# Gated attention output turned by transposing transfers; merge weights staged two column tiles at a time, the output weight in whole rows

## The chip, the cores and the metric

One core of one Trainium2 chip. The metric is the device time in microseconds (us) of one execution of the whole program. The engines are PE (TensorE), DVE (VectorE), ACT (ScalarE), POOL (GpSimd) and SP, which here only issues transfers. SP and POOL each issue their transfers in order from one queue: what stands behind a transfer that still waits for a semaphore waits too.

## The reference

One layer for 2048 prompt tokens and 8 x 4 sample tokens, 1024 wide, float32. The part around the change:

```python
h = rmsnorm(x, g_pre); proj = h @ w_in          # q k v z_a r glu z_b g_a g_b
o, s_new = gla_chunked(q, k, v, log_a, s0)      # 4 heads, dk 128, dv 256
o = rmsnorm(o, g_gla).reshape(bsz, t_len, 1024) # per head, gain of 256 values
y_a = (o * silu(z_a)) @ w_a_out
...                                             # causal depthwise conv, layernorm
y_b = (cv * silu(z_b)) @ w_b_out
merged = sigmoid(g_a) * y_a + sigmoid(g_b) * y_b
x = x + merged @ w_o
x = x + sigmoid(x @ w_pg) * (p @ w_pe)
```

## The kernel before

Matrix products run in float16 with every operand split in a high and a low half, three products for one (`mm3`, lines 263 to 268: high x high, high x low, low x high). A weight comes from memory as float32 into a staging tile `st`, ACT writes the high half (scaled) and DVE the low half (`load_w`, lines 217 and 218).

The stages, in the order of the source:

- Phase 0: x is normalised and turned by PE into `xT` (lines 366 to 371), and the forget gates are computed and stored to `b_d`.
- Attention: four heads one after the other (`gla_head`), each in nine segments, eight of 256 prompt tokens and one of the 32 sample tokens. A head loads six weight tiles (`wq`, `wk`, four `wvz`). A segment projects q, k, v and z, forms the block scores, and multiplies. The normalised, gated output `zz` (line 1069) has tokens on the partitions. PE turns it into PSUM in four 128 x 128 pieces against the identity matrix (line 1075), ACT and DVE scale it by the gain `gsc` and split it into `at` (lines 1079 and 1080), and two stores on POOL's queue write it to `a_d`, which is laid out channel first.
- Convolution: eight channel tiles (`conv_channels`) begin at set segments (`CPOS`); the taps are a long run of DVE instructions (line 504), of lowest priority.
- Fill: 24 gate projections (`gate_w`, `gate_proj`), 120 blocks of 24 matmuls `fl<-xT,wf`, of a priority below the attention. They go to `zz_d`, `ta_d` and `tb_d` and only have to be there when the merge reads them.
- Merge: ten blocks of 208 tokens. For each of eight column tiles, 24 matmuls with `wA` (w_a_out) on `aT`, 24 with `wB` (w_b_out) on `bT`, then DVE multiplies by the gates and adds into `mT`. `load_a` brings `aT` from `a_d`, eight loads for a block into twelve buffers.
- Output: eight pairs of 128-token tiles are multiplied by w_o, and then by w_pg (`halves`). Both weights are used in seven Strassen-like forms of two groups each (`load_forms`): B11, B21, B22 and the sums T1 to T4. For w_o DVE adds the sums in place (line 259); for w_pg accumulating transfers on POOL's queue add them (line 240). `x_d<-x`, the store of the new x, is on POOL's queue too, and the next x is loaded into one of four buffers `x`, so it waits for the store of the x two pairs back.

The order on each engine is not written by hand. A scheduler places the instructions by priorities (`later`) and by its own expected times, and the order is then fixed; within it each engine runs in order. The staging tiles come from one pool:

```python
wst = ctx.enter_context(tc.tile_pool(name="wst", bufs=4))   # tiles of 128 x 1024 float32
```

Of the kernel before, what the change touches and what calls it, by code (L numbers as in the profile page):

```python
# [89 lines left out]
def hybrid_step(ctx: ExitStack, tc, A, O):  # L90
# [2 lines left out]

    cpool = ctx.enter_context(tc.tile_pool(name="const", bufs=1))
    stat = ctx.enter_context(tc.tile_pool(name="stat", bufs=2))
    wst = ctx.enter_context(tc.tile_pool(name="wst", bufs=4))
    wpool = ctx.enter_context(tc.tile_pool(name="wpool", bufs=8))
    slab_ctx = ExitStack()
    slab = slab_ctx.enter_context(tc.tile_pool(name="slab", bufs=8, reuse_waits="tile"))
# [4 lines left out]
    def sb_pool(name, bufs):  # L104
        return tc.tile_pool(name=name, bufs=bufs, reuse_waits="tile")

    def dma(out, in_):
        return nc.sync.dma_start(out=out, in_=in_)
# [37 lines left out]
    def small_vectors(pool):  # L146
        rows = pool.tile([38, P], F32, name="rows", bufs=1)
        dma(rows, A["rows"])
        pt = sm_tile()
        PE.transpose(pt[:, 0:38], rows, ident[0:38, 0:38])  # L150
        V.tensor_copy(vec, pt[:, 0:38])
        V.tensor_scalar(out=g_pre, in0=vec[:, 0:8], scalar1=SX * RSF, scalar2=None, op0=MULT)
        with later(2000):
            V.tensor_scalar(out=gln, in0=vec[:, 16:24], scalar1=RSF, scalar2=None, op0=MULT)
            V.tensor_scalar(out=lnh[:, 0], in0=gln, scalar1=0.5, scalar2=None, op0=MULT)
            V.tensor_scalar(out=lnh[:, 1], in0=b_ln, scalar1=0.5, scalar2=None, op0=MULT)
            V.tensor_scalar(out=gsc, in0=vec[:, 36:38], scalar1=SA * 0.5 * IS * RSF * DK ** -0.5, scalar2=None, op0=MULT)
            V.tensor_tensor(out=sel, in0=ident[:, 0:TD], in1=ident[:, TD:2 * TD], op=ADD)
            for g in range(2, 4):
                V.tensor_tensor(out=sel, in0=sel, in1=ident[:, g * TD:(g + 1) * TD], op=ADD)  # L160
            nc.gpsimd.memset(onesd, 1.0 / D)
# [41 lines left out]
    def wdma(out, in_):  # L203
# [3 lines left out]
        with tc.issue_after(xdma[0].ins):  # L207
            return dma(out, in_)

    def load_w(src, c0, width=P, k0=0, nk=KC, pool=None):  # L210

        c0 = [c0] if isinstance(c0, int) else c0
        w = (pool or wpool).tile([P, 2, nk, len(c0) * width], F16, tag="w", name="w")
        st = wst.tile([P, nk, len(c0) * width], F32, tag="st", name="st")
        for i, c in enumerate(c0):
            wdma(st[:, :, i * width:(i + 1) * width], src[k0 * P:(k0 + nk) * P, c:c + width].rearrange("(k p) c -> p k c", p=P))
        S.activation(w[:, 0], st, AF.Copy, scale=SW)
        V.scalar_tensor_tensor(out=w[:, 1], in0=st, scalar=SW, in1=w[:, 0], op0=MULT, op1=SUB)  # L218
        return w

    def load_forms(src, tiles, accum):


        forms = [[None, None] for _ in range(7)]

        def split(f, g, st):
            w = next(tiles)
            S.activation(w[:, 0], st, AF.Copy, scale=SW)
            V.scalar_tensor_tensor(out=w[:, 1], in0=st, scalar=SW, in1=w[:, 0], op0=MULT, op1=SUB)
            forms[f][g] = w  # L230
        yield forms

        def load(g, r, c, st=None):
            r0 = r * 512 + g * 256
            q = src[r0:r0 + 256, c * 512:(c + 1) * 512].rearrange("(k p) c -> p k c", p=P)
            if st is None:
                st = wst.tile([P, 2, 512], F32, tag="st", name="st")
                dma(st, q)
            else:
                nc.gpsimd.dma_start(out=st, in_=q, accum_op=ADD)  # L240
            return st
        for g in range(2):
            if accum:
                for f, r, c in ((B11, 0, 0), (B21, 1, 0), (B22, 1, 1)):
                    split(f, g, load(g, r, c))
                    yield
                st = load(g, 0, 1)
                for f, r, c in ((T3, 1, 1), (T2, 0, 0), (T4, 1, 0)):
                    split(f, g, load(g, r, c, st))
                    yield  # L250
                split(T1, g, load(g, 0, 0, load(g, 0, 1)))
                yield
                continue
            b11, b21, b22, b12 = (load(g, r, c) for r, c in ((0, 0), (1, 0), (1, 1), (0, 1)))
            for f, st in ((B11, b11), (B21, b21), (B22, b22)):
                split(f, g, st)
                yield
            for f, to, frm in ((T3, b22, b12), (T1, b12, b11), (T2, b11, b22), (T4, b21, b11)):
                V.tensor_tensor(out=to, in0=to, in1=frm, op=ADD)
                split(f, g, to)  # L260
                yield

# [32 lines left out]
    ta_d = dram.tile([P, KC, TT], F32, name="ta_d")  # L295
    tb_d = dram.tile([P, KC, TT], F32, name="tb_d")
    b_d = dram.tile([P, NH, TT], F32, name="b_d")
    a_d = dram.tile([P, KC, 2, TT], F16, name="a_d")

    def gate_w(c, which, other=False, early_w=False):  # L300
        base = (C_ZB, C_GA, C_GB)[which]
# [285 lines left out]


    mpool = ctx.enter_context(sb_pool("mpool", T // (2 * P)))
    wpool2 = ctx.enter_context(sb_pool("wpool2", 9))  # L590
    wA = [load_w(A["w_a_out"][0], c * P) for c in range(KC)]
    w_o = []
    mT = []
    p3_ctx = ExitStack()
    p3 = p3_ctx.enter_context(sb_pool("p3", 2))

    def load_a(a, n, aT, _, __):
        for k in range(KC):
            t = p3.tile([P, 2, DB], F16, tag="aT", name="aT", bufs=12)
            dma(t[:, :, 0:n], a_d[:, k, :, a:a + n])  # L600
            aT.append(t)

    load_a(*ops[0])
    wB = [load_w(A["w_b_out"][0], c * P, pool=wpool2) for c in range(KC)]
    for blk, (a, n, aT, bT, _) in enumerate(ops):
        ahead = iter(())
        if blk + 1 < len(ops):
# [44 lines left out]
    with sb_pool("p4", 2) as p4:  # L652
# [8 lines left out]
        def split_forms(t, sc):  # L661

            a11, a12, a21, a22 = (t[:, 4 * k:4 * k + 4, i * P:(i + 1) * P] for i in range(2) for k in range(2))
            sums = [p4.tile([P, 4, P], F32, tag="sum", name="sum", bufs=3) for i in range(3)]
            F = {f: p4.tile([P, 2, 4, P], F16, tag="f", name="f", bufs=10) for f in (A11, A12, S2, S1, S3, A22, S4)}
            hl(F[A11], a11, sc)
            hl(F[A12], a12, sc)
            V.tensor_tensor(out=sums[0], in0=a21, in1=a22, op=SUB)
# [110 lines left out]
        class Gate:  # L779
# [4 lines left out]
                self.n = [0, 0]  # L784

            def keep(self, X, n):
                r = wst.tile([P, 512], F32, tag="st", name="r")
                S.copy(r, X)
                return r

# [77 lines left out]
def gla_head(tc, nc, A, O, h, L):  # L868
# [13 lines left out]
    for a, n in GSEGS:  # L882
# [184 lines left out]
        rs = rsqrt(ms, nck, ck, 1.0 / DV)  # L1067
        for c in range(nck):
            V.scalar_tensor_tensor(out=zz[:, c], in0=po[0:ck, c], scalar=rs[:, c:c + 1], in1=zz[:, c], op0=MULT, op1=MULT)
        at = p2.tile([P, 2, 2, 256], F16, tag="at", name="at")  # L1070
        pt = sm_tile()
        for j in range(2):
            pj = pt[:, j * 256:j * 256 + n]
            for c in range(nck):
                PE.transpose(pj[:, c * ck:(c + 1) * ck], zz[:, c, j * P:(j + 1) * P], ident[0:ck, 0:ck])
        for j in range(2):
            pj = pt[:, j * 256:j * 256 + n]
            g = L["gsc"][:, j:j + 1]
            S.activation(at[:, j, 0, 0:n], pj, AF.Copy, scale=g)
            V.scalar_tensor_tensor(out=at[:, j, 1, 0:n], in0=pj, scalar=g, in1=at[:, j, 0, 0:n], op0=MULT, op1=SUB)  # L1080
            store(L["a_d"][:, 2 * h + j, :, a:a + n], at[:, j, :, 0:n])
        yield


# [41 lines left out]
```

## Time and profile before

| | |
|---|---|
| median of 3 runs (us) | 2454.31 (2452.01 to 2458.31) |
| the profiled execution's own time (us) | 2464.93 |
| its span in the profile (us) | 2463.2 |
| mean granted TensorE clock | 0.983 |
| PE busy, share of the span | 95% |
| DVE / ACT / POOL busy | 68% / 35% / 18% |

The profiled execution lasted 0.43% longer than the median. Busy time of PE counts matmuls whose ends overlap only once, and a row's mean time of one matmul is longer than the distance to the next.

### The profile page before, as it was taken

The page shows a single profiled execution, that of the slowest core. Times are in us where ns is not written, and L with a number is a line of the kernel's source. Part 1 is how long each engine was busy: PE and PEld are TensorE (multiplying, and loading weights), DVE is VectorE, ACT ScalarE, POOL GpSimd, SP SyncE. Part 2 cuts the span into 40 slices and gives each one's busy share as a digit, 9 for nine tenths or more (in the row PEclk, how much of TensorE's full clock was granted, in tenths as well). Part 3 has the DMA queues.
Part 4 walks back from the last instruction along what each step waited for, and adds up shares of the span by engine and source line. Part 5 has one row for each costly group of instructions (what it writes and reads, how often), then busy time and mean ns, then how long its engine had stood idle before and what let it go on. Part 6 is the DMA issues. An engine that isn't in the chain of part 4 may idle for free.

```text
span 2463.2 us, 43458 instructions
## 1 busy us (share of the span) xinstructions
PE 2336.9 (95%) x16909; PEld 1467.2 (60%) x16909; DVE 1676.1 (68%) x3779; ACT 859.7 (35%) x2043; POOL 451.7 (18%) x1023
## 2 busy tenths in 40 slices
PE   5589999998899999999999989999999998999997
PEld 3245565654456655556655556655999997444544
DVE  6476897496594695594775784654577878865666
ACT  6462123323123324123224223443234334423454
POOL 2011203211112122222122222121000000111333
PEclk9799999999999999999999999999999999999999
DMA  5441201104112113211113130245355445742322
GB/s 182 108 145 32 66 27 61 43 10 125 45 48 63 35 33 111 62 36 51 34 51 94 63 81 29 58 123 166 96 128 130 114 111 181 188 142 89 101 80 73
DMA packets 195942, 210.04 MB, mean 85 GB/s; under 512 B 39323, under 2 KB 167641, under 8 KB 194200
## 3 DMA queue, kind: packets, MB, share of 16 engines
q1 hardware_dynamic: 172104, 133.85, 20.9%
q0 software_dynamic: 23632, 73.42, 8.4%
q8 instruction: 132, 2.16, 0.4%
q14 instruction: 74, 0.61, 0.1%
HBM read 138.33 MB, written 69.72 MB: 84 GB/s over the span
## 4 chain that ended last, share of the span: by engine, by line
PE 74%; DVE 8%; DMA 7%; issue 4%; POOL 4%; ACT 2%; SPq 1%; DVEq 0%; POOLq 0%; ACTq 0%
PE mm L266 13%; PE mm L267 13%; PE mm L268 13%; PE fl L266 6%; PE fl L267 6%; PE fl L268 6%; PE mm L685 4%; PE fl L685 3%; POOL ms L198 1%; DVE acc L504 1%; DMA st<-in_w_in 1%; PE sm L1028 1%; PE sm L1030 1%; PE sm L1029 1%; DMA st<-in_w_pg 1%
## 5 line engine op out<-in xcount | busy, mean ns | idle before, releaser
L266 PE MATMUL mm<-xT,w 128*128 128x416 f16 (+2 forms) x1216 | 362.5, 303 | 4.1 <-DVE zz L932 4.1
L268 PE MATMUL mm<-xT,w 128*128 128x416 f16 (+2 forms) x1216 | 362.4, 303 | 1.0 <-DVE w L218 1.0
L267 PE MATMUL mm<-xT,w 128*128 128x416 f16 (+2 forms) x1216 | 362.3, 303 | 0.0
L266 PE MATMUL fl<-xT,wf 128*128 128x416 f16 x960 | 329.9, 344 | 13.2 <-DVE ob L320 11.7
L267 PE MATMUL fl<-xT,wf 128*128 128x416 f16 x960 | 329.8, 344 | 0.0
L268 PE MATMUL fl<-xT,wf 128*128 128x416 f16 x960 | 329.6, 343 | 0.0
L504 DVE SCALAR_TENSOR_TENSOR acc<-ue,kvec,acc 128x1025 f32<-128x1025 f32 (+1 forms) x232 | 293.9, 1294 | 0.0
L267 PEld LDWEIGHTS <-w 128*128 128x128 f16 x2496 | 243.3, 98 | 69.6 <-issue 11.0
L266 PEld LDWEIGHTS <-w 128*128 128x128 f16 x2496 | 243.4, 98 | 63.2 <-issue 5.5
L268 PEld LDWEIGHTS <-w 128*128 128x128 f16 x2496 | 243.3, 98 | 59.5 <-issue 2.5
L685 PEld LDWEIGHTS <-f 128*128 128x128 f16 x1356 | 132.4, 98 | 160.6 <-issue 6.7
L266 PE MATMUL mm<-w,xT 128*128 128x512 f16 x512 | 195.3, 382 | 0.0
L267 PE MATMUL mm<-w,xT 128*128 128x512 f16 x512 | 195.1, 381 | 0.0
L268 PE MATMUL mm<-w,xT 128*128 128x512 f16 x512 | 195.1, 381 | 0.0
L685 PE MATMUL mm<-wf,f 128*128 128x512 f16 (+1 forms) x780 | 180.2, 379 | 7.3 <-ACT f L658 4.3
L266 PE MATMUL fl<-bT,w 128*128 128x208 f16 x640 | 162.5, 254 | 2.0 <-ACT ob L318 2.0
L266 PE MATMUL mm<-aT,w 128*128 128x208 f16 x640 | 161.5, 253 | 2.4 <-DMA aT<-a_d 2.4
L267 PE MATMUL fl<-bT,w 128*128 128x208 f16 x640 | 162.6, 254 | 0.0
L268 PE MATMUL fl<-bT,w 128*128 128x208 f16 x640 | 162.5, 254 | 0.0
L268 PE MATMUL mm<-aT,w 128*128 128x208 f16 x640 | 161.5, 253 | 0.0
L267 PE MATMUL mm<-aT,w 128*128 128x208 f16 x640 | 161.5, 253 | 0.0
L504 DVE SCALAR_TENSOR_TENSOR acc<-acc,ksum 128x1024 f32<-128x1024 f32 x120 | 155.0, 1292 | 0.0
(277 smaller groups left out, 4061.6 us busy)
## 6 DMA issues: line engine op xcount, KB each, us to landing
x<-in_x_prompt SPq DMA_DIRECT2D x32, 512.0 KB, 6.0
stf<-in_w_in SPq DMA_DIRECT2D x48, 256.0 KB, 6.5
st<-in_w_in SPq DMA_DIRECT2D x24, 512.0 KB, 10.4
zz_d<-ob POOLq DMA_DIRECT2D x40, 208.0 KB, 2.8
ta_d<-ob POOLq DMA_DIRECT2D x40, 208.0 KB, 2.3
tb_d<-ob POOLq DMA_DIRECT2D x40, 208.0 KB, 2.6
cv<-cv_d SPq DMA_DIRECT2D x80, 104.0 KB, 2.1
zz<-zz_d SPq DMA_DIRECT2D x80, 104.0 KB, 2.2
```

The lines of the kernel that those rows point to most:

```text
L198: E.tensor_scalar(out=x, in0=x, scalar1=scale, scalar2=EPS, op0=MULT, op1=ADD)
L266: PE.matmul(out, lhsT=lh, rhs=rh, start=(k == 0), stop=False)
L267: PE.matmul(out, lhsT=lh, rhs=rl, start=False, stop=False)
L268: PE.matmul(out, lhsT=ll, rhs=rh, start=False, stop=(k == nk - 1))
L504: V.scalar_tensor_tensor(out=out[:, 0:n], in0=src[:, j:j + n], scalar=w1[:, j:j + 1], in1=out[:, 0:n], op0=MULT, op1=ADD)
L685: PE.matmul(ps[:, c0:c0 + w], lhsT=F[fa][:, p == 2, k], rhs=W[fb][k // 2][:, p == 1, k % 2, c0:c0 + w], start=start and k + p == 0, stop=k ...
L1028: PE.matmul(po[:, c], lhsT=qe[:, cc], rhs=st_prev, start=True, stop=False)
L1029: PE.matmul(po[:, c], lhsT=att[:, c], rhs=v[:, c], start=first, stop=True)
L1030: PE.matmul(pu[:, c * DV:(c + 1) * DV], lhsT=kdT[:, cc], rhs=v[:, c], start=True, stop=True)
```

## The change

1. The gain of the head norm (`gsc`) moves from `at` into w_a_out: `load_pair` scales w_a_out by `SW * g_gla`.
2. `gla_head` no longer turns `zz` on PE. ACT and DVE split it where it is, tokens on partitions, and two stores write it to `a_d`, now laid out token first.
3. `load_a` reads `a_d` with two transposing transfers of 208 x 1024 float16 for a block, on SP's queue, into one tile of two buffers.
4. `load_pair` stages w_a_out and w_b_out 256 columns at a time (1 MB, runs of 1 KB) in four loads each instead of eight.
5. `load_forms` loads 256 whole rows (1 MB) at a time, two for a group. For w_pg the sums that DVE would add in place are built by seven accumulating transfers for a group, where there were four.
6. The staging pool is two tiles of 128 x 2048 instead of four of 128 x 1024; all other loads (`load_w`) use half of such a tile. A buffer pool of its own holds `r` (`Gate.keep`), `f` has nine buffers instead of ten, `wpool2` eight instead of nine.

```diff
-    wst = ctx.enter_context(tc.tile_pool(name="wst", bufs=4))
+    wst = ctx.enter_context(tc.tile_pool(name="wst", bufs=2))
-            V.tensor_scalar(out=gsc, in0=vec[:, 36:38], scalar1=SA * 0.5 * IS * RSF * DK ** -0.5, scalar2=None, op0=MULT)
+            V.tensor_scalar(out=gsc, in0=vec[:, 36:38], scalar1=SW, scalar2=None, op0=MULT)
+    def st_tile():
+        return wst.tile([P, 2 * D], F32, tag="st", name="st")
+
+    def load_pair(src, c0, pool, gains=None):
+        st = st_tile().rearrange("p (k c) -> p k c", k=KC)
+        dma(st, src[:, c0:c0 + 2 * P].rearrange("(k p) c -> p k c", p=P))
+        for i in range(2):
+            w = pool.tile([P, 2, KC, P], F16, tag="w", name="w")
+            si = st[:, :, i * P:(i + 1) * P]
+            for sl, g in [(slice(0, KC), SW)] if gains is None else [(slice(j, KC, 2), gains[:, j:j + 1]) for j in range(2)]:
+                S.activation(w[:, 0, sl], si[:, sl], AF.Copy, scale=g)
+                V.scalar_tensor_tensor(out=w[:, 1, sl], in0=si[:, sl], scalar=g, in1=w[:, 0, sl], op0=MULT, op1=SUB)
+            yield w
...
-        st = wst.tile([P, nk, len(c0) * width], F32, tag="st", name="st")
+        st = st_tile()[:, 0:nk * len(c0) * width].rearrange("p (k c) -> p k c", k=nk)
...
         for g in range(2):
-            if accum:
-                for f, r, c in ((B11, 0, 0), (B21, 1, 0), (B22, 1, 1)):
-                    split(f, g, load(g, r, c))
-                    yield
-                st = load(g, 0, 1)
-                for f, r, c in ((T3, 1, 1), (T2, 0, 0), (T4, 1, 0)):
-                    split(f, g, load(g, r, c, st))
-                    yield
-                split(T1, g, load(g, 0, 0, load(g, 0, 1)))
...
+            b = []
+            for r in range(2):
+                st = st_tile().rearrange("p (k i c) -> p k i c", k=2, i=2)
+                r0 = r * 512 + g * 256
+                dma(st, src[r0:r0 + 256].rearrange("(k p) (i c) -> p k i c", p=P, i=2))
+                b.append([st[:, :, i] for i in range(2)])
+            for f, r, c in ((B11, 0, 0), (B21, 1, 0), (B22, 1, 1)):
+                split(f, g, b[r][c])
+                yield
+            for f, (r, c), more, done in ((T3, (1, 1), ((0, 1),), (0, 1)), (T1, (0, 1), ((0, 0),), (0, 0)),
+                                          (T2, (0, 0), ((0, 1), (1, 1)), (1, 1)), (T4, (1, 0), ((0, 0), (0, 1), (1, 1)), (0, 0))):
+                to = b[r][c]
+                if accum:
+                    for r1, c1 in more:
+                        r0 = r1 * 512 + g * 256
+                        nc.gpsimd.dma_start(out=to, in_=src[r0:r0 + 256, c1 * 512:(c1 + 1) * 512].rearrange("(k p) c -> p k c", p=P), accum_op=ADD)
+                else:
+                    V.tensor_tensor(out=to, in0=to, in1=b[done[0]][done[1]], op=ADD)
+                split(f, g, to)
+                yield
...
-    a_d = dram.tile([P, KC, 2, TT], F16, name="a_d")
+    a_d = dram.tile([TT, 2, D], F16, name="a_d")
...
-        for k in range(KC):
-            t = p3.tile([P, 2, DB], F16, tag="aT", name="aT", bufs=12)
-            dma(t[:, :, 0:n], a_d[:, k, :, a:a + n])
-            aT.append(t)
+        t = p3.tile([P, 2, KC, DB], F16, tag="aT", name="aT", bufs=2)
+        for i in range(2):
+            nc.sync.dma_start_transpose(out=t[:, i], in_=a_d[a:a + n, i])
+        aT.extend(t[:, :, k] for k in range(KC))
...
-        at = p2.tile([P, 2, 2, 256], F16, tag="at", name="at")
-        pt = sm_tile()
-        for j in range(2):
-            pj = pt[:, j * 256:j * 256 + n]
-            for c in range(nck):
-                PE.transpose(pj[:, c * ck:(c + 1) * ck], zz[:, c, j * P:(j + 1) * P], ident[0:ck, 0:ck])
-        for j in range(2):
-            pj = pt[:, j * 256:j * 256 + n]
-            g = L["gsc"][:, j:j + 1]
-            S.activation(at[:, j, 0, 0:n], pj, AF.Copy, scale=g)
-            V.scalar_tensor_tensor(out=at[:, j, 1, 0:n], in0=pj, scalar=g, in1=at[:, j, 0, 0:n], op0=MULT, op1=SUB)
-            store(L["a_d"][:, 2 * h + j, :, a:a + n], at[:, j, :, 0:n])
+        at = p2.tile([P, 2, 2, DV], F16, tag="at", name="at")[0:ck, :, 0:nck]
+        sc = SA * 0.5 * IS * RSF * DK ** -0.5
+        S.activation(at[:, 0], zz, AF.Copy, scale=sc)
+        V.scalar_tensor_tensor(out=at[:, 1], in0=zz, scalar=sc, in1=at[:, 0], op0=MULT, op1=SUB)
+        for i in range(2):
+            store(L["a_d"][a:a + n, i, h * DV:(h + 1) * DV].rearrange("(c p) v -> p c v", c=nck), at[:, i])
```

The scheduler makes a new order of it. Three places follow. First PE, in the last head, where the eighth segment's decayed keys `kd` are turned (`sm` is PSUM); lines 944 and 966 of before are 953 and 975 of the change. Before:

```order
L266 LDWEIGHTS wf
L266 MATMUL fl<-xT_106,wf 128x416
L1075 MATMUL sm<-ident,zz 128x128
L944 MATMUL sm<-ident,kd 128x128
L1075 MATMUL sm<-ident,zz 128x128 x3
L944 MATMUL sm<-ident,kd 128x128
L966 MATMUL sm<-qk 32x48 x8
L966 MATMUL sm<-eq,kf 32x48 x8
```

The same place after the change:

```order
L277 LDWEIGHTS xT_110
L277 MATMUL mm<-w,xT_110 128x512
L953 MATMUL sm<-ident,kd 128x128 x2
L975 MATMUL sm<-qk 32x48 x8
L975 MATMUL sm<-eq,kf 32x48 x16
```

The four matmuls on `zz` are gone, and no other one stands in their place; ahead of the keys now stands a projection of the attention itself (`mm`) and no fill (`fl`). Through the whole program the fill moves back: before, 2675 of the 2880 fill matmuls stand ahead of the last head's final matmul (L1061); after, 2110 do, and 537 of the others stand in one run between the first 96 `aT` matmuls and the first `bT` matmul.

Second SP's queue at the end of the attention, from the last load of a sample state (`s`) on. Before:

```order
L108 DMA s_16902<-in_state_gla 128x4x256
L108 DMA aT<-a_d 128x2x208 x8
L108 DMA st<-in_w_b_out 128x8x128 x3
L108 DMA aT<-a_d 128x2x208 x2
L108 DMA st<-in_w_b_out 128x8x128
L108 DMA aT<-a_d 128x2x208 x2
```

After:

```order
L108 DMA s_16663<-in_state_gla 128x4x256
L609 DMA_TRANSPOSE aT<-a_d 128x8x208 x3
L108 DMA st<-in_w_b_out 128x8x256
L609 DMA_TRANSPOSE aT<-a_d 128x8x208
L108 DMA st<-in_w_b_out 128x8x256
```

Two whole blocks are brought by four transfers where one block and a half were brought by twelve.

Third POOL's queue in the output stage, with the accumulating transfers of w_pg and the stores of x. Before:

```order
L240 DMA st<-in_w_pg 128x2x512 x2
L111 DMA x_d<-x 128x1024
L240 DMA st<-in_w_pg 128x2x512
L111 DMA x_d<-x 128x1024
L240 DMA st<-in_w_pg 128x2x512
L111 DMA x_d<-x 128x1024 x2
L240 DMA st<-in_w_pg 128x2x512 x2
L111 DMA x_d<-x 128x1024 x4
```

After:

```order
L266 DMA st<-in_w_pg 128x2x512 x2
L111 DMA x_d<-x 128x1024
L266 DMA st<-in_w_pg 128x2x512 x5
L111 DMA x_d<-x 128x1024 x3
L266 DMA st<-in_w_pg 128x2x512
L111 DMA x_d<-x 128x1024
L266 DMA st<-in_w_pg 128x2x512 x2
L111 DMA x_d<-x 128x1024 x2
L266 DMA st<-in_w_pg 128x2x512 x4
L111 DMA x_d<-x 128x1024 x3
```

Runs of five and of four accumulating transfers now stand ahead of stores of x; before, no more than two did.

More of the change, by code (lines that the diff above doesn't have):

```diff
@@ L231, in load_forms @@
         yield forms
[L233 to L241, printed above, removed]
-        for g in range(2):
-            if accum:
-                for f, r, c in ((B11, 0, 0), (B21, 1, 0), (B22, 1, 1)):
-                    split(f, g, load(g, r, c))
-                    yield
-                st = load(g, 0, 1)
-                for f, r, c in ((T3, 1, 1), (T2, 0, 0), (T4, 1, 0)):
-                    split(f, g, load(g, r, c, st))
-                    yield
-                split(T1, g, load(g, 0, 0, load(g, 0, 1)))
-                yield
[L253 to L259, printed above, removed]
@@ L589, in hybrid_step @@
     mpool = ctx.enter_context(sb_pool("mpool", T // (2 * P)))
-    wpool2 = ctx.enter_context(sb_pool("wpool2", 9))
-    wA = [load_w(A["w_a_out"][0], c * P) for c in range(KC)]
+    wpool2 = ctx.enter_context(sb_pool("wpool2", 8))
+    wA = [w for c in range(0, KC, 2) for w in load_pair(A["w_a_out"][0], c * P, wpool, gsc)]
     w_o = []
@@ L597, in load_a @@
     def load_a(a, n, aT, _, __):
-        for k in range(KC):
-            t = p3.tile([P, 2, DB], F16, tag="aT", name="aT", bufs=12)
-            dma(t[:, :, 0:n], a_d[:, k, :, a:a + n])
-            aT.append(t)
+        t = p3.tile([P, 2, KC, DB], F16, tag="aT", name="aT", bufs=2)
+        for i in range(2):
+            nc.sync.dma_start_transpose(out=t[:, i], in_=a_d[a:a + n, i])
+        aT.extend(t[:, :, k] for k in range(KC))
     load_a(*ops[0])
-    wB = [load_w(A["w_b_out"][0], c * P, pool=wpool2) for c in range(KC)]
+    wB = [w for c in range(0, KC, 2) for w in load_pair(A["w_b_out"][0], c * P, wpool2)]
     for blk, (a, n, aT, bT, _) in enumerate(ops):
@@ L664, in split_forms @@
             sums = [p4.tile([P, 4, P], F32, tag="sum", name="sum", bufs=3) for i in range(3)]
-            F = {f: p4.tile([P, 2, 4, P], F16, tag="f", name="f", bufs=10) for f in (A11, A12, S2, S1, S3, A22, S4)}
+            F = {f: p4.tile([P, 2, 4, P], F16, tag="f", name="f", bufs=9) for f in (A11, A12, S2, S1, S3, A22, S4)}
             hl(F[A11], a11, sc)
@@ L786, in keep @@
             def keep(self, X, n):
-                r = wst.tile([P, 512], F32, tag="st", name="r")
+                r = p4.tile([P, 512], F32, tag="r", name="r", bufs=3)
                 S.copy(r, X)
```

## The prediction

> **What bounds the kernel now.** I read the page's head first, then the stages, then what PE waits for.
>
> ```profile
> span 2463.2 us, 43458 instructions
> PE 2336.9 (95%) x16909; PEld 1467.2 (60%) x16909; DVE 1676.1 (68%) x3779; ACT 859.7 (35%) x2043; POOL 451.7 (18%) x1023
> ...
> PE 74%; DVE 8%; DMA 7%; issue 4%; POOL 4%; ACT 2%; SPq 1%; DVEq 0%; POOLq 0%; ACTq 0%
> ```
>
> The stages, as stretches of time (busy us of PE, PEld, DVE, ACT, POOL, then clock and DMA): start, attention, its end, merge, output by w_o, output by w_pg.
>
> ```profile
> 0.00:215.00 215.00, 157.23 (x897) 86.62 (x898) 115.82 (x205) 109.77 (x183) 31.73 (x95) 0.91 0.42 128
> 215.00:1580.00 1365.00, 1324.90 (x9371) 780.83 (x9369) 954.15 (x2080) 398.27 (x1102) 294.78 (x686) 0.99 0.19 54
> 1580.00:1720.00 140.00, 135.42 (x940) 78.37 (x939) 76.59 (x217) 63.23 (x149) 29.99 (x70) 0.99 0.46 136
> 1720.00:2060.00 340.00, 336.09 (x3676) 330.89 (x3674) 255.01 (x834) 122.67 (x286) 1.62 (x3) 0.99 0.46 119
> 2060.00:2180.00 120.00, 113.37 (x652) 57.61 (x651) 98.61 (x153) 47.17 (x69) 13.94 (x16) 0.97 0.69 196
> ```
>
> PE is the bound: 97% busy in the attention, 99% in the merge, and three quarters of the chain. So PE work taken away is worth its time; work taken from ACT, DVE or POOL only what PE waited for it. PE is idle 126 us in all, 58 of them in the first 215 us. What it waited for outside the start and near the change:
>
> ```profile
> PE sm L1075 <- DVE zz L1069: 14.6, 8, 2.9
> PE fl L266 <- DVE ob L320: 11.7, 8, 4.0
> PE sm L1052 <- DMA s<-in_state_gla: 9.7, 1, 9.7
> ...
> PE mm L266 <- DMA aT<-a_d: 2.4, 3, 1.4
> ```
>
> **The transposes on PE go.** The group of full segments, and instructions of PE in order of time, two of the fill (`fl`) ahead of four transposes (start us, us):
>
> ```profile
> L1075 PE MATMUL sm<-ident,zz 128*128 128x128 f32 x128 | 25.5, 287 | 14.6 <-DVE zz L1069 14.6
> ...
> 905.80 0.34 PE L267 MATMUL fl<-xT,wf 128*128 128x416 f16 x1
> 905.98 0.34 PE L268 MATMUL fl<-xT,wf 128*128 128x416 f16 x1
> 907.57 0.33 PE L1075 MATMUL sm<-ident,zz 128*128 128x128 f32 x1 [1.25 <-DVE zz L1069]
> 907.73 0.27 PE L944 MATMUL sm<-ident,kd 128*128 128x128 f32 x1
> 907.96 0.55 PE L1075 MATMUL sm<-ident,zz 128*128 128x128 f32 x3
> ```
>
> 128 instructions keep PE busy 25.5 us. Started back to back they cost less: three span 0.55 us and one lasts about 0.27, so the distance is (0.55 - 0.27) / 2 = 0.14 us, and 128 of them 18 us. I take 24, ends 18 and 25.5; the eight small ones of the sample segments are within that.
>
> In front of them PE waited 14.6 us for `zz`, which hangs on POOL's slow reciprocal root. After the change nothing on PE reads `zz`, so the wait itself is gone. Late next are the keys, scores and state matmuls. They ran here behind the transposes, with runs of 20 to 60 fill matmuls as cover; the new order has 565 fewer fill matmuls inside the attention. I take 9 of the 14.6, ends 0 and 14.6.
>
> **ACT and DVE in the attention.** Per full segment two 480 ns splits out of PSUM become one of 512 columns:
>
> ```profile
> L1079 ACT ACTIVATE at<-sm,gsc 128x256 f16<-128x256 f32 x64 | 30.4, 475 | 55.1 <-PE sm L1075 46.2 <-DVE at L1080 8.4
> L1080 DVE SCALAR_TENSOR_TENSOR at<-sm,gsc,at 128x256 f16<-128x256 f32 x64 | 30.7, 480 | 11.9 <-ACT at L1079 11.7 <-ACT zz L931 0.2
> ...
> DVE zz L1069 <- POOL rsq_y L190: 112.2, 31, 6.4
> ...
> L659 DVE SCALAR_TENSOR_TENSOR f<-sum,f 128x512 f16<-128x512 f32 x64 | 42.8, 686 | 0.0
> ```
>
> By the last row (a split of 512 columns elsewhere) DVE goes from 30.7 to 32 x 0.69 = 22 us, ACT alike; both lie beside PE: nothing. POOL still issues two stores of 128 KB a segment. Yet DVE is 954 / 1365 = 70% busy in the attention, and if the same work runs in some 120 us less (565 fill matmuls at the 0.18 us between the two rows above, 100 us, and the transposes), it is near 76%. That is the cover that could fail (second rival).
>
> **The transposing transfers.** No row shows one. The nearest:
>
> ```profile
> aT<-a_d SPq DMA_DIRECT2D x80, 104.0 KB, 2.4
> x<-x_d SPq DMA_DIRECT2D x16, 512.0 KB, 4.2
> st<-in_w_in SPq DMA_DIRECT2D x24, 512.0 KB, 10.4
> ...
> 1697.59 3.99 SPq L108 DMA_DIRECT2D aT<-a_d  x8
> 1694.61 0.71 POOL L111 DMA_DIRECT2D a_d<-at  x1
> ...
> L266 PE MATMUL mm<-aT,w x640: 249/253/253, 1701.8 to 2072.7; 128*128 128x208 f16 x160
> L1061 PE MATMUL sm<-oq,sel x8: 379/391/403, 674.0 to 1681.2; 128*32 128x256 f32 x8
> ```
>
> A transfer now has 416 KB. Bounds: 2.4 us, as the small plain ones, to 10.4 us, as 512 KB in short runs; I take 5, nearest to the 512 KB row with long runs. In the merge a block of PE work lasts about 340 / 10 = 34 us and the next block's two transfers are issued ahead of it, so they hide, and SP's eight issues (3.99 us) fall to two. The 2.4 us that PE waited for the later half of `aT` go.
>
> Exposed is the first block. The first load follows the last store of the attention by 3.0 us and PE starts on `aT` 20.6 us after L1061 (1681.2 to 1701.8). In the new order 74 fill matmuls at 0.18 us, 13 us, lie between the two. The path without the PE transposes is about 4 us shorter than the 16.4 us to the issue, so 12, plus two transfers in turn, 10: 22 us against 13. The fill run may be stretched by some 3 us of evictions; I take +6, ends 0 and +20 (10.4 us each). With the 2.4: +3.6.
>
> The Trainium skill, page "VectorE: DVE Perf Modes", section "The three transpose paths", speaks against the change: 1309 ns for a 128 x 128 block by the DMA crossbar, 390 ns by TensorE. Our row has 287 ns for the PE's. At that price a transfer of 13 such blocks would be an estimated 17 us, and the first block's term some +30 instead of +6. The page "DMA: Bandwidth & Descriptors", section "Latency and other measured facts", gives 261 GB/s for such transfers, an estimated 1.6 us. No run so far shows which holds.
>
> **The staging.** w_a_out and w_b_out come in eight loads of 1 MB instead of sixteen of 512 KB, and are split in as many bytes; w_a_out takes 16 splits of half the width instead of eight, eight more instructions on ACT and on DVE, beside fill: nothing. In phase 0 ACT's queue has the weight splits between those of `xT`, and the third and fourth loads now wait until a staging tile is free:
>
> ```profile
> 78.22 1.06 ACT L217 ACTIVATE w<-st 128x1024 f16<-128x1024 f32 x1 [3.77 <-DMA st<-in_w_in]
> 87.72 1.06 ACT L217 ACTIVATE w<-st 128x1024 f16<-128x1024 f32 x1 [5.87 <-DMA st<-in_w_in]
> 97.88 1.06 ACT L217 ACTIVATE w<-st 128x1024 f16<-128x1024 f32 x1 [6.80 <-DMA st<-in_w_in]
> ```
>
> These waits hold `xT` and PE. Two tiles make the loads later, but the new order puts three splits ahead of the next `xT` instead of four. Taken at 0, ends -5 and +10.
>
> **The output stage.** For w_pg POOL issues 14 accumulating transfers of 512 KB instead of 8; those on one tile follow each other, and the stores of x stand behind them.
>
> ```profile
> 2110.08 1.19 POOL L240 DMA_DIRECT2D st<-in_w_pg  x1 [2.26 <-DVE wf L229]
> 2117.90 0.59 POOL L111 DMA_DIRECT2D x_d<-x  x1 [6.64 <-DMA st<-in_w_pg]
> 2132.16 0.56 POOL L111 DMA_DIRECT2D x_d<-x  x1 [8.06 <-DVE x L765]
> ...
> x_d<-x POOLq DMA_DIRECT2D x16, 512.0 KB, 4.5
> ...
> DVE gfin L655 <- DMA gfin<-in_g_final: 2.9, 1, 2.9
> ```
>
> One that is waited for holds the queue some 8 us (1.19 + 6.64). The run of five has three such waits within its two tiles, about 21 us, so the next store of x comes some 20 us later than here. The load two pairs on needs it; store and load land in 4.5 + 4.2 us, so that x is there 29 us later than it was stored before, and a pair lasts 14 us (2117.90 to 2132.16), two 28: a hole of 0 to 8 us, and a smaller one at the run of four. w_pg itself is due only when the w_o pairs end, 100 us on. Against it the load of `gfin`, for which DVE waits 2.9 us (in a stage where DVE is 98.61 / 120 busy), is issued earlier. I take +3, ends -3 and +20. That two 1 MB tiles of w_o must be free before the second group loads is inside these ends.
>
> **The sum.** -24 - 9 + 3.6 + 0 + 3 = -26.4 us. Against the profiled execution, 2464.93, that is 2438.5; it stands 10.6 us above the median of the three runs (2454.31), so against the median 2428.
>
> **Rivals.**
> - The cover holds better: all 14.6 us go and the first block costs nothing. 18 to 25.5 and 14.6 and 2.4 give 2412 to 2419; with the better ends of phase 0 and output, 2404.
> - The waits come back in the attention: PE, with fewer fill matmuls, waits for DVE and ACT. For it speaks DVE at 76% and the 112.2 us that it waits for POOL's root; against it that PE waits only some 40 us in the attention now. If it loses 12 us, 2440.
> - Staging and POOL take it all: phase 0 at +10, output at +20. 2454.3 - 33 + 3.6 + 30 = 2455: no change. For it: ACT's waits for staged weights above, and the order of POOL; against it: w_pg is due late, and the order of ACT is no worse.
> - Slower: the transfers starve the merge. With T for one transfer, the first block costs 12 + 2T - 13 us and each of nine later blocks 2T - 34 where that is above 0. At T = 17 us the first block takes the whole gain of 33 us and the time is 2454; from there it is slower, at T = 20 us 2454.3 - 33 + 39 + 9 x 6 = 2514. For it: nothing here shows a transposing transfer. Against: 512 KB landed in 4.2 to 10.4 us. The 1309 ns of the Trainium skill's page on VectorE lies just on this edge.
>
> **How the numbers follow.** Runs of this kernel differ by 0.3%, 7 us, about what can be told from no change: faster is below 2447, slower above 2462. The sum 0.56 (2418 to 2438); better 0.08; waits back 0.14, of it 0.12 faster; all taken 0.12, of it 0.09 the same; starved 0.10, of it 0.08 slower. Faster 0.56 + 0.08 + 0.12 = 0.76, same 0.02 + 0.09 + 0.02 = 0.13, slower 0.03 + 0.08 = 0.11. The range 2404 to 2458 leaves out the starved merge and parts of the ends.
>
> **What would show it.** L1075 gone and PE's busy time near 2312 us; PE's wait for `zz` gone and no new one of its size in the attention; DMA_TRANSPOSE landing in about 5 us; a wait of PE for `aT` once, under 10 us; stores of x behind the accumulations by some 20 us. The prediction is wrong if a transfer takes over 15 us, or if PE's idle time grows by more than 15 us.

## The result, and the profile after

The changed kernel takes 2436.78 us (median of six runs, 2430.26 to 2442.99) against 2455.39 us for the kernel before beside it: a ratio of 0.9924, 95% interval 0.9900 to 0.9948, so 19 us less (13 to 25). The prediction was 2428 us in a range of 2404 to 2458. Sign and size came out; the experiments below show that they did so in good part for other reasons than the working gave.

The head of the changed kernel's page (its profiled execution took 2438.05 us, 1.3 above the median):

```profile
span 2436.3 us, 42955 instructions
...
PE 2326.4 (95%) x16773; PEld 1452.8 (60%) x16773; DVE 1670.9 (69%) x3751; ACT 854.3 (35%) x2015; POOL 470.1 (19%) x1029
```

PE's busy time fell by 10.5 us, to 2326.4 and not to the 2312 that the prediction named as its sign, and its idle time by 16.4 (from 126.3 to 109.9). The stages of the changed kernel, busy us of PE, PEld, DVE, ACT, POOL, then clock and DMA; they end earlier than before, and the third now holds the first block of the merge:

```profile
0.00:215.00 215.00, 167.26 (x970) 92.41 (x971) 123.61 (x218) 110.78 (x187) 36.24 (x105) 0.94 0.41 127
215.00:1450.00 1235.00, 1211.18 (x8580) 708.34 (x8578) 925.86 (x1986) 372.27 (x1019) 286.62 (x647) 0.99 0.20 56
1450.00:1600.00 150.00, 137.54 (x1023) 82.15 (x1022) 95.91 (x292) 76.76 (x194) 34.84 (x78) 0.98 0.48 134
1600.00:2040.00 440.00, 439.15 (x4341) 393.54 (x4338) 256.90 (x828) 130.50 (x294) 13.50 (x25) 1.00 0.42 104
2040.00:2160.00 120.00, 107.43 (x504) 45.76 (x505) 96.87 (x143) 45.95 (x68) 22.91 (x25) 0.91 0.78 207
```

In the start PE works 10 us more than before in the same 215 us. Between 1450 and 1600 us it idles 12.5 us, where the kernel before idles 8.0. In the 120 us from the end of the merge on PE is busy for 107 us at a clock of 0.91 (before, from 2075 us on, 113 at 0.97). What PE waited for, all of its larger waits but those of the start:

```profile
PE fl L275 <- DVE ob L329: 10.7, 7, 2.7
...
PE mm L694 <- ACT f L667: 7.7, 1, 7.7
PE fl L275 <- ACT ob L327: 6.9, 1, 6.9
...
PE sm L1052 <- ACT att L1010: 4.7, 2, 4.1
PE mm L694 <- DVE x L774: 4.1, 1, 4.1
...
PE sm L1061 <- DMA s<-in_state_gla: 2.2, 1, 2.2
```

The 14.6 us for `zz` are gone. Longer than before are the waits for one eviction of the fill by ACT (`ob`: 6.9 us, before 2.0) and two in the output stage (for `f` 7.7 us, before 4.3; for `x` 4.1 us at one time, before 1.7 at three). The tile `aT`, its first and last matmul and its transfers (ns, minimum, median and maximum that one held SP's queue), and who waited for them:

```profile
L275 PE MATMUL mm<-aT,w x640: 249/253/253, 1559.1 to 2036.9; 128*128 128x208 f16 x160
...
L609 SPq DMA_TRANSPOSE aT<-a_d x20: 1444/2048/5817, 1553.7 to 1970.7; - x20
...
  PE mm L275: 1.1, 1
...
DMA to landing us min/median/max: 4.1/5.3/9.8
```

They land in 5.3 us in the median, and PE waited 1.1 us for them in all. The merge begins 143 us earlier than before (1559.1 against 1701.8) and in the midst of the fill: 143 us ahead of the fill's end, where it was 30. SP's and ACT's queues there:

```profile
1553.67 6.50 SPq L609 DMA_TRANSPOSE aT<-a_d  x3
1560.28 0.53 SPq L108 DMA_DIRECT2D st<-in_w_b_out  x1
1560.87 5.82 SPq L609 DMA_TRANSPOSE aT<-a_d  x1
```

```profile
1567.73 2.00 ACT L221 ACTIVATE w<-st 128x1024 f16<-128x1024 f32 x2 [9.11 <-DMA st<-in_w_b_out]
...
1588.60 0.38 ACT L574 ACTIVATE bT<-th 128x208 f16<-128x208 f32 x1 [9.27 <-DVE th L571]
...
1591.40 0.49 ACT L327 ACTIVATE ob<-fl 128x416 f32<-128x416 f32 x1
```

ACT stands 9.1 us for a staged weight and 9.3 us for `th`, with the evictions of the fill behind both; the one at 1591.40 is what PE waits 6.9 us for. `th` itself stood on DVE behind a sum that waited for a load of `cv`, the convolution's output for a later block of the merge:

```profile
1587.75 0.38 DVE L538 TENSOR_TENSOR s<-s,cv 128x208 f32<-128x208 f32 x1 [8.02 <-DMA cv<-cv_d]
1588.19 0.38 DVE L571 TENSOR_TENSOR th<-th,zz 128x208 f32<-128x208 f32 x1
```

A load of `cv` lands in 2.1 us in the median; of those issued between 1560 and 1600 us one took 10.7 us, and the two loads of w_o beside them (1 MB each) 15.7 us in the median. The second place is POOL's queue in the output stage:

```profile
2078.48 1.18 POOL L266 DMA_DIRECT2D st<-in_w_pg  x1 [0.33 <-DVE wf L244]
2086.53 1.18 POOL L266 DMA_DIRECT2D st<-in_w_pg  x1 [6.87 <-DMA st<-in_w_pg]
2093.32 1.20 POOL L266 DMA_DIRECT2D st<-in_w_pg  x1 [5.61 <-DMA st<-in_w_pg]
2094.04 1.09 POOL L111 DMA_DIRECT2D x_d<-x  x1
```

The run of accumulations holds the store of x until 2094.04. Counted from the end of the merge that is 12 us later than before (2117.90 us, less the 35.8 us by which the merge ended earlier, is 2082).

### The profile page after: what moved, and what is told of

It reads as the page before. It is cut to its first block, busy times and chain, and to the rows that moved or that the text cites. A ratio compares the mean times of both kernels' runs of the same rounds, so it can differ in the third digit from the quotient of the medians.

```text
span 2436.3 us, 42955 instructions
## 1 busy us (share of the span) xinstructions
PE 2326.4 (95%) x16773; PEld 1452.8 (60%) x16773; DVE 1670.9 (69%) x3751; ACT 854.3 (35%) x2015; POOL 470.1 (19%) x1029
## 4 chain that ended last, share of the span: by engine, by line
PE 76%; DVE 8%; DMA 5%; POOL 5%; issue 3%; ACT 2%; SPq 1%; DVEq 0%; POOLq 0%; ACTq 0%
PE mm L275 13%; PE mm L277 13%; PE mm L276 13%; PE fl L275 6%; PE fl L276 6%; PE fl L277 6%; PE mm L694 6%; PE fl L694 4%; DVE acc L513 2%; DMA st<-in_w_in 2%; DMA stf<-in_w_in 1%; POOL rsq_t L187 1%; PE sm L1038 1%; PE sm L1037 1%; POOL rsq_t L188 1%
## 5 line engine op out<-in xcount | busy, mean ns | idle before, releaser
L275 PE MATMUL fl<-xT,wf 128*128 128x416 f16 x960 | 329.7, 343 | 20.2 <-DVE ob L329 10.7
L513 DVE SCALAR_TENSOR_TENSOR acc<-ue,kvec,acc 128x1024 f32<-128x1024 f32 (+1 forms) x232 | 293.1, 1283 | 0.0
```

The costliest lines, as they stand in the source:

```text
L275: PE.matmul(out, lhsT=lh, rhs=rh, start=(k == 0), stop=False)
L513: V.scalar_tensor_tensor(out=out[:, 0:n], in0=src[:, j:j + n], scalar=w1[:, j:j + 1], in1=out[:, 0:n], op0=MULT, op1=ADD)
```

## Experiments

The differences below are between ratios to the kernel before, times 2455 us; the bounds of a difference of two ratios are put together from their intervals.

**The two halves apart.** The turn alone: parts 1 to 3 of the change, with `load_w` scaling w_a_out and the staging as before. The staging alone: the changed kernel with the turn undone.

```diff
 # turn only, on the kernel before
-    def load_w(src, c0, width=P, k0=0, nk=KC, pool=None):
+    def load_w(src, c0, width=P, k0=0, nk=KC, pool=None, gains=None):
-    wA = [load_w(A["w_a_out"][0], c * P) for c in range(KC)]
+    wA = [load_w(A["w_a_out"][0], c * P, gains=gsc) for c in range(KC)]
 # and gla_head, load_a, a_d, gsc as in the change
```

Expected of the turn alone:

> The kernel before with the turn alone: the gated output is split in its own orientation, stored as rows and turned by the transposing transfers, with the gain in w_a_out; staging stays in four tiles of 4 KB a partition, with the old order of loads and eight accumulations for w_pg. Theory (the turn is the gain, the staging costs about as much in the output stage as it brings in phase 0): the start as before (first matmul on xT near 115 us, not 103), the output stage as before (388 us, not 397), the attention shorter by 18 to 25 us of transposes and some of the 14.6 us of wait: 2425 to 2435 against 2455 for the kernel before, so level with the changed kernel or up to 10 us below. Rival A (a good part of the changed kernel's gain is the earlier start): 2440 to 2448, above the changed kernel. Rival B (staging only costs, nothing in phase 0 is kept): 2415 to 2425.

Expected of the staging alone:

> The changed kernel with the turn put back on PE: transposes, splits out of PSUM, the turned a_d and its plain loads as in the kernel before; the staging stays new (two tiles of 8 KB, column tiles in pairs, whole rows, fourteen accumulations). Theory: first matmul on xT near 103 us instead of 115, output stage near 397 us instead of 388, the two cancel: 2450 to 2460, no change that can be told from the kernel before. Rival A: the earlier start is kept to the end and the output stage costs less than it seems: 2440 to 2448. Rival B: staging only costs: 2460 to 2470.

The turn alone: 2431.34 us, ratio 0.9899 (0.9880 to 0.9917), -25 us. That is in the theory's band, but the start is not as before: the first matmul `mm<-xT,w` comes at 106.7 us, where 115 was expected. The staging alone: 2442.17 us, 0.9945 (0.9929 to 0.9961), -14 us, in the band of its rival A. Both together -19. On the new staging the turn is worth 5 us (±7), which cannot be told from nothing, on the old one 25 (±5). Either half makes a new order (by the traces the staging alone moves over 800 of PE's 16909 matmuls), and in the order of the staging alone PE, which still turns `zz`, waits for it much less:

```profile
PE sm L1084 <- DVE zz L1078: 4.4, 5, 1.5
```

**What a transpose on PE costs.** The turn put back on PE in vain, beside the transfers; and, on the kernel before, each transpose issued three times.

```diff
 # turn twice, on the changed kernel
+        pt = sm_tile()
+        for j in range(2):
+            pj = pt[:, j * 256:j * 256 + n]
+            for c in range(nck):
+                PE.transpose(pj[:, c * ck:(c + 1) * ck], zz[:, c, j * P:(j + 1) * P], ident[0:ck, 0:ck])
 # three times, on the kernel before
+                for _ in range(3):
                     PE.transpose(pj[:, c * ck:(c + 1) * ck], zz[:, c, j * P:(j + 1) * P], ident[0:ck, 0:ck])
```

> The changed kernel with the old transposes of the gated output put back on PE into a PSUM tile that nobody reads: the transfers turn the output, as in the changed kernel, and PE does so too in vain. Theory (what the change saves is PE's work on the transposes, 18 to 25 us, and PE's wait for the gated output in front of them, up to 14.6 us): 20 to 35 us slower than the changed kernel, 2457 to 2472, with the wait of PE for zz back at 10 to 15 us. Rival (the matmuls behind had to wait for other things anyway, so that the transposes were free): under 12 us slower.

> The kernel before with each of the 136 transposes of the gated output issued three times into the same place: 272 more on PE, no new wait. It prices a transpose on PE. By the spacing of 0.14 us between transposes issued back to back: +37 us (2493). By the mean duration of one, 0.2 us: +53 us. Rival (most of them stand in time in which PE waits anyhow, as putting them back in vain cost 5 us in place of 18): +10 to +20 us.

In vain: 2441.66 us, 0.9943 (0.9928 to 0.9959), 5 us (±7) above the changed kernel; the rival held. Three times: 2488.47 us, 1.0139 (1.0119 to 1.0159), +34 us (±5). The page's line of PE there:

```profile
PE 2363.5 (95%) x17181; PEld 1495.8 (60%) x17181; DVE 1676.3 (67%) x3779; ACT 859.4 (35%) x2043; POOL 435.9 (18%) x1023
```

272 more transposes are 34 us of time, 0.125 us each, and 26.6 to 29.4 us of PE's busy time (against the two profiles of the kernel before), 0.10 to 0.11 us each. So by this run the 136 of the kernel before cost 13 to 17 us (up to 20 with the interval), and the 37 us that the spacing of 0.14 us gave lie within the interval. The run in vain shows a third of it: 5 us (±7) of time, and PE's busy time only 0.9 us above the changed kernel's. But it is not the changed kernel with more work. By the traces over 2000 of PE's matmuls stand elsewhere in it than in the changed kernel, and its merge begins at 1666.8 us, not at 1559.1. So it does not price the transposes; the three-fold run has a new order too (some 750 matmuls moved), so its price is the better one and still not a clean one.

**The kernel before once more, and two tiles.** To see whether the waits of the first profile were chance; and the kernel before with two staging tiles for the column tiles and nothing else.

```diff
 # two tiles, on the kernel before
-    wst = ctx.enter_context(tc.tile_pool(name="wst", bufs=4))
+    wst = ctx.enter_context(tc.tile_pool(name="wst", bufs=2))
+    wsf = ctx.enter_context(sb_pool("wsf", 2))        # opened at the merge
-                st = wst.tile([P, 2, 512], F32, tag="st", name="st")
+                st = (wsf if c else wst).tile([P, 2, 512], F32, tag="st", name="st")
-                r = wst.tile([P, 512], F32, tag="st", name="r")
+                r = wsf.tile([P, 512], F32, tag="st", name="r")
```

> The kernel before, unchanged, for a second profile of it and for what two timings of one program can differ by. So far the turn alone gave -25 us and the staging alone -14 us, yet both together -19 us. Theory A (the kernel before has waits that any new order of its attention closes): the second profile shows the start (last matmul on rw at 106 to 110 us) like the others, so that the 114 us of the first profile is chance, and again about 10 to 15 us of wait for zz in front of the transposes and about 10 us for the state of the decode segment. Theory B (chance of the one profile): zz below 8 us and the state below 5 us as in the kernel with the staging alone, and the start again near 108 us. Time: the ratio within 0.3% of 1 by both.

> The kernel before with nothing changed but the staging tiles: two instead of four for the column tiles (the four half-row tiles of the output stage are two of these and two of their own). The turn stays on PE, loads stay single, whole rows are not used. Theory A (the gain of the staging alone is the order that follows from two tiles, in the start and through the attention): 2430 to 2440, that is the 2442 us of the staging alone less the 6 to 9 us that its output stage costs. Theory B (the pairs of column tiles or something at the merge brings it): 2450 to 2458, as the kernel before.

> The turn alone and the two staging tiles of the run beside it, the output stage as in the kernel before: all of the change but the pairs of column tiles and the whole rows. Theory A (two tiles and the turn close the same waits, so that their gains do not add; the whole rows cost 6 to 9 us in the output stage): 2425 to 2433, level with the turn alone (2431) and 4 to 12 us below the changed kernel. Theory B (the two gains add and the pairs or the rows take them away): 2412 to 2422.

The kernel before again: 2456.32 us, 0.9996 (0.9983 to 1.0010). Two tiles: 2429.53 us, 0.9889 (0.9872 to 0.9905), **-27 us from the staging tiles alone**. The turn and two tiles: 2423.65 us, 0.9868 (0.9853 to 0.9883). Theory A held, though not in all its numbers: in the repeated profile the last matmul on `rw` still comes at 112.1 us, so the late start was not chance, and the wait for the state is 6.7 us in place of 10; both times lie a little below its bands. The wait for `zz` in the repeated profile, with the number of waits and the longest:

```profile
PE sm L1075 <- DVE zz L1069: 14.9, 8, 2.7
```

and the evictions that begin each of the attention's segments there (ns of one, then first and last start in us):

```profile
L931 ACT ACTIVATE zz<-mm x68: 357/378/418, 221.2 to 1625.3; 128x256 f32<-128x256 f32 x64, 32x256 f32<-32x256 f32 x4
```

The same two with two tiles:

```profile
PE sm L1076 <- DVE zz L1070: 7.2, 5, 2.1
```

```profile
L932 ACT ACTIVATE zz<-mm x68: 356/378/414, 200.5 to 1592.4; 128x256 f32<-128x256 f32 x64, 32x256 f32<-32x256 f32 x4
```

The attention starts 21 us earlier, and half of the wait for `zz` goes without the turn being touched. PE idles 18 us less than in the repeated profile of the kernel before (99.0 against 117.4): 6.5 in the first 215 us, 5 in the next 1235, 7 in the rest. It is the order of the whole program that changes: by the traces at least 767 of PE's 16909 matmuls stand elsewhere, where the two profiles of the kernel before have one order. The two halves of the change close some of the same waits, so their gains do not add.

**Pairs and whole rows.** The version with the turn and two tiles is all of the change but the pairs and the whole rows, and it is 14 us (±7) faster than all of it. The changed kernel without pairs tells the two apart:

```diff
-    wA = [w for c in range(0, KC, 2) for w in load_pair(A["w_a_out"][0], c * P, wpool, gsc)]
+    wA = [load_w(A["w_a_out"][0], c * P, gains=gsc) for c in range(KC)]
-    wB = [w for c in range(0, KC, 2) for w in load_pair(A["w_b_out"][0], c * P, wpool2)]
+    wB = [load_w(A["w_b_out"][0], c * P, pool=wpool2) for c in range(KC)]
```

> The changed kernel with single column tiles of w_a_out and w_b_out (sixteen loads of 512 KB) in place of pairs; the whole rows of w_o and w_pg and their fourteen accumulations stay. The changed kernel stands 13 us above the version without pairs and rows (2436.8 against 2423.7). Theory A (the rows cost it in the output stage, about 8 us by the profiles, and the pairs cost the rest at the start of the merge): 2430 to 2434. Rival B (the rows cost all of it): 2435 to 2439. Rival C (the pairs cost nearly all): 2422 to 2427.

2444.87 us, 0.9961 (0.9947 to 0.9976): none of the three. The rows cost 23 us (±5), with the tiles of 128 x 2048, the accumulations and the pool sizes that come with them, and the pairs give 9 (±7) back. Where the attention begins in this version:

```profile
L946 ACT ACTIVATE zz<-mm x68: 356/378/384, 217.3 to 1520.2; 128x256 f32<-128x256 f32 x64, 32x256 f32<-32x256 f32 x4
```

217.3 us, and 215.4 in the changed kernel, against 199.1 with the turn and two small tiles: the early start is mostly gone. From the last matmul on `aT` to the end, the five profiles with rows and accumulations show 396 to 400 us, the eight with the old output stage 390 to 396. So some 6 us of the rows' price lie in the output stage and the rest ahead of it. Why a larger tile gives the scheduler an order that starts later is open.

**The sums of w_pg by DVE.**

```diff
-                steps = load_forms(A["w_pg"][0], halves8, True)
+                steps = load_forms(A["w_pg"][0], halves8, False)
```

> The changed kernel, but the four sums of each half of w_pg are made by DVE in the staging tiles instead of by accumulating transfers on POOL's queue (none of the fourteen is left; eight more DVE additions). Theory (the runs of up to five accumulations keep the stores of x and ACT's splits waiting, about 4 us of PE's wait and a dip of the clock behind it): the output stage falls from 397 to 389 to 394 us, the time by 3 to 8 us. Rival A (DVE is the tight engine at the hole and eight additions cost it more): the same or up to 5 us slower. Rival B (the output stage's loss is the late second half of w_o alone): within 2 us of the changed kernel.

2437.25 us, 0.9925 (0.9909 to 0.9941): level with the changed kernel (0 ± 7 us), as its rival B said of the time. Its profile does show the hole closed. 20 us of the output stage, from 42 us after the merge's end, in the changed kernel:

```profile
2079.20:2099.20 20.00, 15.93 (x67) 6.68 (x65) 13.29 (x20) 5.66 (x8) 4.02 (x5) 0.86 0.86 162
```

and with the sums by DVE:

```profile
2084.20:2104.20 20.00, 19.72 (x93) 8.87 (x91) 20.00 (x28) 7.83 (x12) 1.60 (x3) 1.00 0.41 138
```

PE's 4.1 us of idling and the clock of 0.86 are gone, and the last stage is 391.8 us instead of 399.3. But this profile reached the end of the merge 5 us later in nearly the same order, and the median confirms nothing; the gain is not shown in the time.

**The new hole at the start of the merge.** In all eight kernels in which PE no longer turns, it idles 8 to 12 us between 1500 and 1600 us; in those where it does, 0 to 2. The merge begins later in the latter; counted from 70 us before it begins to 40 us after, it is 9 to 15 us against 2 to 6. These 100 us in the kernel before (second profile), in the version with the turn and two tiles, and what ACT waits for in the latter:

```profile
1500.00:1600.00 100.00, 100.00 (x844) 60.58 (x842) 57.41 (x201) 46.30 (x126) 19.00 (x62) 1.00 0.20 58
```

```profile
1500.00:1600.00 100.00, 90.39 (x542) 52.67 (x541) 56.48 (x143) 42.45 (x92) 20.33 (x46) 0.95 0.66 180
```

```profile
ACT w L223 <- DMA st<-in_w_b_out: 14.1, 5, 9.8
```

Three runs ask whether the transposing transfers make it: the loads of w_b_out on POOL's queue; plain transfers of as many bytes, which leave the output unturned; and each transfer issued twice.

```diff
 # w_b_out on POOL's queue, on the turn with two tiles (load_w takes the issuer as "via")
+    wB = [load_w(A["w_b_out"][0], c * P, pool=wpool2, via=store) for c in range(KC)]
 # plain transfers, on the same
-            nc.sync.dma_start_transpose(out=t[:, i], in_=a_d[a:a + n, i])
+            dma(t[:, i].rearrange("p k t -> p (k t)")[:, 0:KC * n], a_d[a:a + P].rearrange("t i d -> t (i d)")[:, 0:KC * n])
 # twice, on the changed kernel
+            for _ in range(2):
                 nc.sync.dma_start_transpose(out=t[:, i], in_=a_d[a:a + n, i])
```

> The version with the turn and two tiles, without pairs and rows (2423.7 us), with the eight loads of w_b_out issued on POOL's queue, not behind the transposing transfers on SP's. Theory (the transposing transfers hold SP's queue, the loads of w_b_out behind them come late, ACT waits for them with evictions of the fill behind, and PE waits 9.6 us for such an eviction): PE's idle time between 1500 and 1600 us falls from 9.6 to under 4 us and the time by 4 to 9 us, to 2415 to 2420. Rival (the wait there is for something else, or stores on POOL's queue now come late instead): no change or slower, 2422 to 2430.

> The version with the turn and two tiles (2423.7 us) with the twenty transposing transfers replaced by plain ones of as many bytes, 128 runs of 3.3 KB each: the gated output arrives unturned, so that the merge multiplies by the wrong columns; all else is the same work in nearly the same order. Theory (the transposing transfers cost next to nothing where they stand, and the 9 to 12 us that PE idles between 1500 and 1600 us in every kernel with the turn is the work that the order bunches at the merge's early start): 2420 to 2425, PE's idle time there still 8 to 12 us. Rival (the transfers hold SP's queue for 2 to 6 us each and their traffic delays the weights, so that they make the idle time): 2412 to 2418, and PE's idle time there under 4 us.

> The changed kernel with each transposing transfer issued twice, the second over the first: 40 instead of 20. Theory (in the merge two transfers hide under 34 us of matmuls; exposed is the first block, some 5 us a transfer, and the loads of w_b_out behind it): 5 to 15 us slower, 2442 to 2452, with the merge after its first block as long as before. Rival A (all is hidden): within 3 us. Rival B (the transfers starve the merge, as the fourth rival of the prediction has it): over 25 us slower, with PE waiting for aT at most blocks.

On POOL's queue: 2419.19 us, 0.9860 (0.9840 to 0.9880), 2 us (±6) less than the version it was made from. The time lies in the theory's band, but the hole stays, and so does ACT's wait; that the place of these loads on SP's queue makes them is refuted:

```profile
1500.00:1600.00 100.00, 91.00 (x531) 51.98 (x529) 55.39 (x141) 39.60 (x87) 25.77 (x53) 0.95 0.64 173
```

```profile
ACT w L223 <- DMA st<-in_w_b_out: 16.8, 5, 8.4
```

Plain transfers: 2416.16 us, 0.9848 (0.9825 to 0.9870), 5 us (±7) less: the time in the rival's band, the idle time in the theory's, for again the hole stays. The transfers there, the 100 us, and ACT's wait:

```profile
L108 SPq DMA_DIRECT2D aT<-a_d x20: 320/424/1257, 1532.9 to 1960.9; - x20
DMA to landing us min/median/max: 3.5/4.2/9.3
```

```profile
1500.00:1600.00 100.00, 91.09 (x520) 51.87 (x519) 55.85 (x143) 40.77 (x87) 19.70 (x45) 0.93 0.61 178
```

```profile
ACT w L223 <- DMA st<-in_w_b_out: 13.0, 5, 6.9
```

So in this version the turning in the transfer is not what makes the hole; it costs at most some 12 us, and by the profile 1.2 us of landing (5.4 against 4.2) and 1.7 us of SP's queue for each. Issued twice: 2445.89 us, 0.9970 (0.9957 to 0.9984), 11 us (±7) more, as the theory said, with PE waiting 0.4 us for `aT`; the merge is not starved. What is common to all the kernels with the hole is that the merge begins in the midst of the fill, with the last loads of w_b_out, the first of w_o and the merge's own inputs (`cv` among them) bunched there: DMA is 0.61 to 0.73 busy in these 100 us, against 0.07 to 0.30 in the others. Where PE has a long wait there, it hangs on one of these transfers, and not always on the same one: in the version with the turn and two tiles and the two runs made from it ACT's evictions stand behind splits of w_b_out; in the changed kernel the wait hangs on `cv`, as shown above, and likewise with the turn alone (DVE waits 9.5 us for `cv` there and PE 6.7 us behind it) and without pairs (8.2 and 10.2). All this is read from the traces; no run took the bunching away.

## Why the prediction came out

- **The transposes, -24:** mis-sized. By the three-fold run they cost 13 to 17 us; the working took nearly the mean duration of one (0.20 us of busy time). Its lower end, 0.14 us from start to start, is above the 0.10 to 0.125 of that run but within the interval of its time.
- **The wait for `zz`, -9 of 14.6:** the wait is gone in the changed kernel, and no wait of its size came in the attention. It was real (14.9 us in the second profile), but not bound to the turn: two staging tiles alone take half of it, the new staging two thirds.
- **ACT and DVE beside PE, 0:** held. The split of `zz` takes 23.7 us on DVE, where 22 were worked out, and PE's idle time from 215 to 1450 us fell from 32.1 to 23.8 us.
- **The transfers, 5 us each:** held; 5.3 us. The rival in which they starve the merge fell with it. The Trainium skill, page "VectorE: DVE Perf Modes", section "The three transpose paths", had spoken for that rival; here 13 blocks of 128 x 128 landed in 5.3 us, which is 0.41 us a block and not the 1309 ns of that page.
- **The first block, +6:** not seen. PE waited 1.1 us for the first `aT`, and the 2.4 us for the later ones went. Of the 10 us that it idles there, 6.9 stand behind bunched transfers and the evictions after them, which the prediction had not seen. From 1450 us to the merge's end PE still idles no longer than in the kernel before (12.8 us against 16.5 and 13.5).
- **The staging, 0:** this is the step that failed. "The order of ACT is no worse" looked at three splits in the start. The number of tiles moves the order of the whole program, which is worth -27 us for two tiles, and -14 for the staging as changed. PE idles 10.0 us less in the first 215 us of the changed kernel than in the first profile of the kernel before, 7.2 less than in the second.
- **The output stage, +3 (-3 to +20):** about +6 by the means of the profiles, +9 by the changed kernel's own, inside the ends. Stores of x came 12 us late where 20 were said; the pause in PE is there, and the second half of w_o is late as well. In the changed kernel ACT's split of it waited 7.6 us:

```profile
2032.99 1.06 ACT L243 ACTIVATE wf<-st 128x1024 f16<-128x1024 f32 x1 [7.59 <-DMA st<-in_w_o]
```

The time of a profile is PE's busy time plus its idle time, so three pairs of profiles show what the turn did on each staging (us, with the turn less without it; the kernel before by its second profile; the merge's end is the last matmul on `aT`):

| turn on | span | PE busy | idle to 215 | to 1450 | to the merge's end | after it |
|---|---|---|---|---|---|---|
| old staging | -25.4 | -14.8 | -3.3 | -8.6 | 0.0 | +1.3 |
| two tiles | -6.5 | -6.0 | -2.9 | -4.5 | +7.6 | -0.8 |
| new staging | +0.7 | -3.3 | -2.2 | -1.8 | +6.7 | +1.3 |

Each is one profile, up to 5 us off its median; the ratios give -25 (±5), -5 (±5) and -5 (±7). On the old staging the turn saves as much busy time as the three-fold run prices (13 to 17 us) and closes waits in the attention besides, and the hole costs nothing net, because the kernel before idles as long (13.5 us) on its own way from 1450 us to the merge's end. With two tiles, small or large, these waits are short already (4.9 and 6.0 us there), and the hole takes back what the turn gains. Why PE's busy time falls by 3 to 15 us for the same 136 transposes is open.

The forecast of -26 was near -19 because the gain of the turn, put too high (-33, where it is worth 5 ± 7 on the new staging), stood in for that of the staging, which was missed (-14). That the two came to nearly the same sum is luck.

## What to carry to other kernels

Before a gain is put down to the work that a change removes, run its side edits by themselves: here a pool of two tiles instead of four, a detail of the change, is worth 27 us where the whole change is worth 19, and the version with the turn and two tiles and without whole rows beats both kernels (0.9868 of the kernel before, 14 us under the changed one). Where a scheduler sets the order, a wait in the profile belongs to that order and not to the instruction that stands behind it, so count on PE only the work itself. Price it by adding some rather than by its mean duration, and first see that the order stayed: the two runs here that added transposes gave 0.125 and under 0.04 us for each, and neither kept its order. And when a stage begins earlier, ask which weights and evictions it now meets there.

## What was not expected of the hardware

- A transposing transfer of 208 x 1024 float16 holds SP's queue for 2.05 us in the median and up to 5.8 us; a plain one of as many bytes 0.42 us, up to 1.3.
- Accumulating transfers of 512 KB landed in 6.4 us (median of 8) in the kernel before and 7.6 us (of 14) in the changed one, where more follow each other on one tile.
- Idling often came with a lower granted clock: 4.1 us of it in 20 us of the output stage with 0.86, where the filled stretch had 1.00. It is no rule that these runs show: with the transfers issued twice PE idled 7.5 us between 1500 and 1600 us at a clock of 1.00.
